# Ones in TensorE's pauses, pinned casts, and a residual kept in accumulators: a two-layer trunk in fp32

## Chip, cores and metric

One core of one Trainium2 chip runs the whole program. The metric is device time in microseconds (us) of one execution; a shorter time is better.

## The reference, cut to what matters

Two layers on a prompt of 1024 tokens and a sample of 512, 1024 features wide. Layer 0 mixes tokens with a Fourier transform, layer 1 with attention; each is followed by a SwiGLU. The change touches layer 0 alone.

```python
def rms_norm(x, g):
    y = xf * lax.rsqrt(jnp.mean(xf * xf, axis=-1, keepdims=True) + EPS)
    return (y * g).astype(x.dtype)
...
def fourier_mixer(x, g, w):
    h = rms_norm(x, g).reshape(b, s, N_FGROUPS, FGROUP_DIM)
    mixed = jnp.real(jnp.fft.fft2(h, axes=(1, 3), norm="ortho"))
    return mixed.reshape(b, s, d) @ w
...
def swiglu_ffn(x, g, w_gate, w_up, w_down):
    h = rms_norm(x, g)
    return (jax.nn.silu(h @ w_gate) * (h @ w_up)) @ w_down
...
x = x + fourier_mixer(x, ...)      # layer 0; attention_mixer in layer 1
x = x + swiglu_ffn(x, ...)
```

## The kernel before

Tokens are worked on in three blocks of 512 columns: block 0 is the sample ("s"), blocks 1 and 2 the prompt ("p"). Activations are transposed: features on the 128 partitions, in eight chunks `dc` or `n`, tokens along the free dimension. Each fp32 operand is split into a high part (a cast to fp32r) and a low part (the source minus the cast), and each product is three matmuls, high by high, high by low and low by high (`mm3`, L244 to L246). So each weight of 128x1024 passes through four steps (`weights`, L248): SP issues its load into a `raw` buffer, ScalarE (ACT) casts it, GpSimd (POOL) subtracts, TensorE (PE) uses both parts. There are few `raw` buffers; a load waits until POOL's subtraction has freed one. The projection's weights (`folded`, L586) pass through one step more: POOL adds and subtracts the two halves of a chunk of `wf` (L590, L591) ahead of the cast.

The start runs in these stages. `load_rows("s")` loads the sample. `lead` (L1079) is the sample's mixer: squares and their sums on ACT, the reciprocal root on VectorE (DVE) in `rsqrt` (L257, here 15 small operations, with the square root's iterations written out), then four quarters of features. In each, rows of tokens are scaled and combined (ACT L424, DVE L426, cast L237), multiplied by the transform `mat_s` on PE, and turned over the group's features (`dd`, `alt`, L498, L405). The transform's matrices come in one staging buffer; `mat_p`, the prompt's, comes in it too, by a DMA that ACT issues in the first microsecond, and ACT casts it in four parts (L1088). `lead` also begins four folds, and with fold 2 the small matrix `w64`.

`follow` (L1098) is the projection: for each of eight chunks 25 matmuls of 256 or 258 columns into four PSUM tiles, which DVE adds to the chunk of the residual (L624, L625, L629). `new_residual` (L294) writes the chunk to `xres` in DRAM, squares it on ACT (L305) and adds the squares up on DVE (L306). After the last chunk `rstd_cols` (L276) sums over partitions by products with ones (L280) and calls `rsqrt`; `normed` (L311) spreads the factors over partitions by four products of a diagonal with ones (L288, L289), loads each chunk of `xres` back, multiplies it on DVE into PSUM (L324) and splits it with the gain (ACT L240, DVE L241) into `h`.

Then `ffn(0, 0)` runs 22 steps `fc`: eight chunks of gate, eight of up (48 matmuls of 512 columns each step with `part`), the SwiGLU, and eight chunks of down, whose sums DVE adds to accumulators in SBUF; at the first step these are loaded from `xres` (L663). Beside it, `weave` (L1028) runs an auxiliary stage, here the prompt's mixer `x_0`. It alternates between the two by the costs that each `yield` states. Later stages pair the other blocks' SwiGLU with attention in the same way.

What `weave` lays down is the program; a scheduler of the framework sets from it a fixed order of instructions for each engine, by its own estimates of when each could start. `keep_in_program_order`, which the change uses, pins an instruction to its place in the program's order. The chip then runs each engine's list strictly in order, and an instruction that waits holds up all behind it. DMA issues stand in the lists of SP and ACT alike.

## Time and profile before

| | us |
|---|---|
| median of 3 runs | 3134.45 |
| lowest, highest | 3128.28, 3134.93 |
| profiled execution | 3136.16 |
| its span | 3134.4 |
| PE busy in the span | 3005.0 (96%) |
| DVE, POOL, ACT busy | 1656.4, 1325.6, 1243.9 |

The span is what the profiler shows of the execution; busy times are sums over each engine's instructions. An engine's idle time is shown in front of the instruction that ended it, with the event that released it. PE's clock is shown twice: as the clock that was granted in a stretch, and in how closely products follow each other.

### The profile page before, as it was taken

The page shows a single profiled execution, that of the slowest core. Times are in us where ns is not written, and L with a number is a line of the kernel's source. Part 1 is how long each engine was busy: PE and PEld are TensorE (multiplying, and loading weights), DVE is VectorE, ACT ScalarE, POOL GpSimd, SP SyncE. Part 2 cuts the span into 40 slices and gives each one's busy share as a digit, 9 for nine tenths or more (in the row PEclk, how much of TensorE's full clock was granted, in tenths as well). Part 3 has the DMA queues.
Part 4 walks back from the last instruction along what each step waited for, and adds up shares of the span by engine and source line. Part 5 has one row for each costly group of instructions (what it writes and reads, how often), then busy time and mean ns, then how long its engine had stood idle before and what let it go on. Part 6 is the DMA issues. An engine that isn't in the chain of part 4 may idle for free. (4 is left out here: it accounts for less than half of the span.)

```text
span 3134.4 us, 37508 instructions
## 1 busy us (share of the span) xinstructions
PE 3005.0 (96%) x14382; PEld 2471.0 (79%) x14382; DVE 1656.4 (53%) x2974; ACT 1243.9 (40%) x1807; POOL 1325.6 (42%) x616
## 2 busy tenths in 40 slices
PE   5699999999999999999999999999999999999999
PEld 5687788888887778888878788778787777777777
DVE  5664455453466553453455466665337455655556
ACT  5443323233266632233334377777424222222221
POOL 3444734444233454444443322222546644554452
PEclk9799999999999999999999999999999999999999
DMA  5424553333223454343343311111645511111111
GB/s 181 157 81 119 178 173 103 115 117 95 82 91 99 164 174 133 125 132 105 98 155 92 103 58 65 58 58 58 203 141 176 182 54 54 48 48 53 54 48 61
DMA packets 131385, 336.13 MB, mean 107 GB/s; under 512 B 15699, under 2 KB 23891, under 8 KB 130693
## 3 DMA queue, kind: packets, MB, share of 16 engines
q1 hardware_dynamic: 129476, 322.68, 32.2%
q10 hardware_dynamic: 1440, 6.85, 0.6%
q0 software_dynamic: 288, 4.19, 0.4%
q8 instruction: 113, 1.85, 0.2%
q14 instruction: 68, 0.55, 0.1%
HBM read 286.48 MB, written 47.19 MB: 106 GB/s over the span
## 5 line engine op out<-in xcount | busy, mean ns | idle before, releaser
L238 POOL TENSOR_TENSOR w<-raw,w 128x1024 fp32r<-128x1024 f32 (+1 forms) x463 | 1093.4, 2371 | 1632.9 <-ACT w L237 1596.3
L237 ACT CAST w<-raw 128x1024 fp32r<-128x1024 f32 (+1 forms) x463 | 479.2, 1038 | 754.8 <-PE c L246 357.2
L664 DVE TENSOR_TENSOR acc<-c,acc 128x512 f32<-128x512 f32 x704 | 482.8, 689 | 476.2 <-PE c L246 473.0
L244 PE MATMUL g<-h,w 128*128 128x512 f32 x1408 | 557.2, 396 | 6.8 <-DVE h L241 6.5
L246 PE MATMUL g<-h,w 128*128 128x512 f32 x1408 | 553.7, 394 | 0.0
L245 PE MATMUL g<-h,w 128*128 128x512 f32 x1408 | 552.9, 393 | 0.0
L244 PE MATMUL c<-mid,w 128*128 128x512 f32 x1056 | 419.9, 399 | 17.3 <-DVE acc L664 15.2
L245 PE MATMUL c<-mid,w 128*128 128x512 f32 x1056 | 414.5, 393 | 0.7 <-DVE mid L238 0.7
L246 PE MATMUL c<-mid,w 128*128 128x512 f32 x1056 | 413.9, 392 | 0.0
L771 DVE TENSOR_TENSOR acc<-c,acc 128x512 f32<-128x512 f32 x352 | 240.9, 689 | 192.8 <-PE c L246 192.0
L244 PEld LDWEIGHTS g<-h,w 128*128 128x128 f32 x1408 | 266.1, 189 | 59.7 <-DVE h L241 6.8
L246 PEld LDWEIGHTS g<-h,w 128*128 128x128 f32 x1408 | 266.0, 189 | 55.1 <-POOL w L238 0.3
L245 PEld LDWEIGHTS g<-h,w 128*128 128x128 f32 x1408 | 266.2, 189 | 52.1
L244 PEld LDWEIGHTS c<-mid,w 128*128 128x128 f32 x1056 | 198.6, 189 | 80.1 <-DVE acc L664 27.4
L246 PEld LDWEIGHTS c<-mid,w 128*128 128x128 f32 x1056 | 199.0, 188 | 41.5
L245 PEld LDWEIGHTS c<-mid,w 128*128 128x128 f32 x1056 | 199.5, 189 | 40.2 <-DVE mid L238 1.8
L244 PE MATMUL c<-h,w 128*128 128x512 f32 x480 | 189.9, 396 | 1.7 <-ACT h L237 1.7
L245 PE MATMUL c<-h,w 128*128 128x512 f32 x480 | 188.5, 393 | 1.3 <-POOL h L238 1.3
L246 PE MATMUL c<-h,w 128*128 128x512 f32 x480 | 187.2, 391 | 0.0
L983 DVE TENSOR_REDUCE col<-a 128x1 f32<-128x1024 f32 (+1 forms) x96 | 100.4, 1045 | 125.9 <-PE a L246 125.7
L987 ACT ACTIVATE p<-a,col,rqc 128x1024 f32<-128x1024 f32 (+1 forms) x96 | 102.3, 1066 | 65.7 <-DVE col L984 65.3
L689 ACT ACTIVATE t<-g 128x512 f32<-128x512 f32 x88 | 52.6, 598 | 175.4 <-PE g L246 175.1
(299 smaller groups left out, 4749.9 us busy)
## 6 DMA issues: line engine op xcount, KB each, us to landing
raw<-in_down_dram SPq DMA_DIRECT2D x110, 512.0 KB, 3.7
raw<-in_gate_dram SPq DMA_DIRECT2D x88, 512.0 KB, 3.7
raw<-in_up_dram SPq DMA_DIRECT2D x88, 512.0 KB, 3.8
raw<-in_qkv_dram SPq DMA_DIRECT2D x36, 512.0 KB, 3.5
t<-xres SPq DMA_DIRECT2D x64, 256.0 KB, 4.2
xres<-t SPq DMA_DIRECT2D x48, 256.0 KB, 3.7
acc<-xres SPq DMA_DIRECT2D x48, 256.0 KB, 4.3
raw<-in_wo_dram SPq DMA_DIRECT2D x24, 512.0 KB, 4.3
```

Source lines behind the costliest of these rows:

```text
L237: act.copy(hi, src)
L238: eng.tensor_tensor(lo, src, hi.bitcast(F32), op=ALU.subtract)
L244: pe.matmul(out, lh, rh, start=first, stop=False)
L245: pe.matmul(out, lh, rl, start=False, stop=False)
L246: pe.matmul(out, ll, rh, start=False, stop=last)
L664: dve.tensor_tensor(acc[dc], ps, acc[dc], op=ALU.add)
L689: act.activation(s, ga, AF.Silu)
L771: dve.tensor_tensor(acc, ps, acc, op=ALU.add)
L983: dve.tensor_reduce(st[:, 0:1], s_in, op=ALU.max, axis=AX.X)
L987: act.activation(p, s_in, AF.Exp, bias=st[:, 1:2], scale=rqc[:, gq, h : h + 1], accum_out=sm[:, 0:1])
```

## The change

It has eight parts, all in the stages ahead of, and at, the first SwiGLU's first step.

1. A dummy Square on ACT at the very start.
2. `busy(n)`: n products of a 128x128 tile of ones with itself, whose results nothing reads, pinned: 64 behind `load_rows("s")`, 10 behind the last chunk of the projection, 12 behind the column sums.
3. `rsqrt` keeps its iterate in an SBUF column and drops four copies.
4. The DMA of `dft_p` (2 MB) moves from ACT's queue at the start to SP's behind the first combination; the gate is a one-element copy on DVE into the staging buffer (`after`). The four casts of `mat_p` and the folds move to later, stated places `k` of `lead`, where their casts are pinned; the first fold has such a gate too.
5. Folds 4 to 7 are begun in the projection ahead of their chunk, and the gate, up and down weights of step 0 at its chunks 5, 6 and 7.
6. Block 0's residual stays in the accumulators of `ffn(0, 0)` (`resident`): nothing is written to `xres` nor read back.
7. Its norm is one DVE operation per chunk (accumulator by gain by factor, into SBUF), ACT's cast, and POOL's subtraction.
8. In step 0 gate and up alternate chunk by chunk, and `x_0` is advanced four times instead of once ahead of `follow`.

In the rows of order below, a name ends in the number of its tile, `<-` separates what is written from what is read.

**ACT at the sample's last combination** (`comb`, the cast that the fourth quarter's products wait for; `eo` are casts for the projection's operand, x_p prompt rows), before:

```order
L237 CAST xrs_526<-t_524 1x256
L424 ACTIVATE a_495<-x_136,r_s 128x256
L240 ACTIVATE spec_s<-g_471,gains 128x2
L355 DMA x_p_626<-in_rows_p_dram 128x1024
L237 CAST comb_494<-a_495 128x2x256
L237 CAST eo_196<-c_501 128x256
L237 CAST eo_196<-c_502 128x256
```

and now, where w_525 is the fourth fold:

```order
L457 ACTIVATE a_555<-x_138,r_s 128x256
L241 ACTIVATE spec_s<-g_526,gains 128x2
L238 CAST xrs_588<-t_586 1x256
L238 CAST eo_257<-c_561 128x256
L238 CAST eo_257<-c_562 128x256
L635 CAST w_525<-raw_521 128x1024
L238 CAST comb_554<-a_555 128x2x256
```

The fourth fold's cast has come to stand directly ahead of the combination's.

**POOL in the projection** (L590 and L591, now L629 and L630, are the add and subtract of a fold; L238 and L636 the low part of a weight; w_970 and w_885 the last chunk's), before:

```order
L591 TENSOR_TENSOR raw_874<-raw_873 128x512
L238 TENSOR_TENSOR w_878<-raw_874,w_878 128x1024
L590 TENSOR_TENSOR raw_920<-raw_919 128x512
L591 TENSOR_TENSOR raw_920<-raw_919 128x512
L238 TENSOR_TENSOR w_924<-raw_920,w_924 128x1024
L590 TENSOR_TENSOR raw_966<-raw_965 128x512
L591 TENSOR_TENSOR raw_966<-raw_965 128x512
L238 TENSOR_TENSOR w_970<-raw_966,w_970 128x1024
L238 TENSOR_TENSOR w_1101<-raw_1099,w_1101 128x1024
L238 TENSOR_TENSOR w_1131<-t_1141,w_1131 128x2x256
L238 TENSOR_TENSOR w_1106<-raw_1104,w_1106 128x1024
```

and now (w_794 and w_800 are folds 4 and 5, the w of two pieces belong to the prompt's mixer):

```order
L636 TENSOR_TENSOR w_794<-raw_790,w_794 128x1024
L636 TENSOR_TENSOR w_800<-raw_796,w_800 128x1024
L629 TENSOR_TENSOR raw_881<-raw_880 128x512
L629 TENSOR_TENSOR raw_837<-raw_836 128x512
L630 TENSOR_TENSOR raw_837<-raw_836 128x512
L630 TENSOR_TENSOR raw_881<-raw_880 128x512
L239 TENSOR_TENSOR w_744<-t_754,w_744 128x2x256
L239 TENSOR_TENSOR w_744<-t_759,w_744 128x2x256
L636 TENSOR_TENSOR w_841<-raw_837,w_841 128x1024
L239 TENSOR_TENSOR w_767<-t_777,w_767 128x2x256
L239 TENSOR_TENSOR w_767<-t_782,w_767 128x2x256
L636 TENSOR_TENSOR w_885<-raw_881,w_885 128x1024
```

The folds no longer alternate one by one, and four of the prompt's subtractions have come in between.

**ACT between the last chunk's square and the norm's diagonals** (L305, now L330, squares a chunk; L288, now L308, makes a diagonal; w_1101, w_1106 and w_1111 are gate, up and down of step 0 and w_1339 the gate of step 1), before:

```order
L237 CAST w_1106<-raw_1104 128x1024
L305 ACTIVATE a_1008<-t_973 128x512
L237 CAST w_1111<-raw_1109 128x1024
L237 CAST w_1131<-t_1146 128x2x256
L424 ACTIVATE c_1161<-x_p_626,r_p 128x256
L424 ACTIVATE c_1250<-x_p_626,r_p 128x256
L237 CAST w_1339<-raw_1337 128x1024
L237 CAST w_1160<-t_1170 128x2x256
L237 CAST w_1160<-t_1175 128x2x256
L237 CAST xrs_1191<-t_1187 1x256
L424 ACTIVATE c_1250<-x_p_626,r_p 128x256
L288 ACTIVATE t_1036<-ident,rs_1011 128x128
```

and now (w_1002, w_1041, w_1082 and w_1427 in their place):

```order
L330 ACTIVATE a_1036<-acc_788 128x512
L276 CAST w_1002<-raw_1000 128x1024
L330 ACTIVATE a_1077<-acc_788 128x512
L276 CAST w_1041<-raw_1039 128x1024
L330 ACTIVATE a_1129<-acc_788 128x512
L238 CAST xrs_1231<-t_1227 1x256
L276 CAST w_1082<-raw_1080 128x1024
L276 CAST w_1427<-raw_1425 128x1024
L308 ACTIVATE t_1167<-ident,rs_1132 128x128
L308 ACTIVATE t_1170<-ident,rs_1132 128x128
```

The cast of step 1's gate, which stood well ahead of the diagonals, now stands right in front of them, behind that of down.

The diff, cut to its core:

```diff
+    act.activation(col(1), ones[:, 0:1], AF.Square)
...
+    def busy(n):
+        o = bankg()
+        for _ in range(n):
+            pinned(pe.matmul(o[:, 0:P], ones, ones, start=True, stop=True))
+    def after(dst, src):
+        dve.tensor_copy(dst[0:1, 0:1], src[0:1, 0:1])
...
+        pinned(act.copy(flat[:, 0], raw)) if early else act.copy(flat[:, 0], raw)
+        pool.tensor_tensor(flat[:, 1], raw, flat[:, 0].bitcast(F32), op=ALU.subtract)
...
-        v, ti, a, z = (scr[:, k * n : (k + 1) * n] for k in range(4))
-        vs, zs = col(n), col(n)
+        v, ti, a = (scr[:, k * n : (k + 1) * n] for k in range(3))
+        z = col(n)
         dve.tensor_scalar(v, x, scale, EPS, op0=ALU.mult, op1=ALU.add)
         dve.tensor_scalar(ti.bitcast(I32), v.bitcast(I32), 1, None, op0=ALU.logical_shift_right)
         dve.tensor_scalar(z.bitcast(I32), ti.bitcast(I32), -1.0, MAGIC, op0=ALU.mult, op1=ALU.add)
-        dve.tensor_copy(vs, v)
-        dve.tensor_copy(zs, z)
         for k in range(3):
-            dve.tensor_tensor(a, z, zs, op=ALU.mult)
-            dve.scalar_tensor_tensor(a, a, -0.5, vs, op0=ALU.mult, op1=ALU.mult)
-            if k < 2:
-                dve.scalar_tensor_tensor(z, a, 1.5, zs, op0=ALU.add, op1=ALU.mult)
-                dve.tensor_copy(zs, z)
-            else:
-                dve.scalar_tensor_tensor(y, a, 1.5, zs, op0=ALU.add, op1=ALU.mult)
+            dve.tensor_tensor(a, v, z, op=ALU.mult)
+            dve.scalar_tensor_tensor(a, a, -0.5, z, op0=ALU.mult, op1=ALU.mult)
+            dve.scalar_tensor_tensor(z if k < 2 else y, a, 1.5, z, op0=ALU.add, op1=ALU.mult)
...
+        if first and not resting:
+            resting.append(True)
+            busy(12)
...
+        if not stays:
+            sp.dma_start(xres[b][:, dc, :], piece)
...
+        if b in resident:
+            for dc in range(NC):
+                x = tmp()
+                dve.scalar_tensor_tensor(x, resident[b][dc], gain[:, dc : dc + 1], r, op0=ALU.mult, op1=ALU.mult)
+                split(h[:, 0, dc], h[:, 1, dc], x, eng=pool)
+            got["h"] = h
+            return
...
-        split(flat[:, 0], flat[:, 1], f.rearrange("p k n -> p (k n)"), eng=pool)
-        return w
-    def mixer_projection(seq, done, ready=()):
+        f = f.rearrange("p k n -> p (k n)")
+        pinned(act.copy(flat[:, 0], f))
+        pool.tensor_tensor(flat[:, 1], f, flat[:, 0].bitcast(F32), op=ALU.subtract)
+        yield
+    ahead, begun = [], []
+    def begin_fold(n, tag, later=None):
+        begun.append(folded(n, tag, later))
+        ahead.append(next(begun[-1]))
...
+            if two:
+                w, _ = folded(n, "wX")
+            else:
+                w = ahead.pop(0)
+                for m in (4, 5) if n == 0 else (n + 5,) if n < 3 else ():
+                    cur[0] = "XF"[m % 2]
+                    begin_fold(m, "wF")
+                cur[0] = "F"
+                if n in (1, 2, 4, 5):
+                    next(begun.pop(0))
+                if n >= 5:
+                    early.append(weights_by((t["gate"], t["up"], t["down"])[n - 5][0, 0]))
+                    first[n - 5] = next(early[-1])
+                if n >= 6:
+                    next(early[n - 6])
...
+                if not two and n == NC - 1:
+                    busy(10)
...
+        here = b in resident
+        acc = resident.pop(b) if here else accumulators()
...
+            if here and fc == 0:
+                wg, wu, wd = (first[i] for i in range(3))
+            else:
+                wg, wu, wd = (weights(t[v][layer, fc]) for v in ("gate", "up", "down"))
             ga, up = bankg(), bankg()
             for dc in range(NC):
                 part(wg, h, ga, dc)
+                if here and fc == 0:
+                    part(wu, h, up, dc)
...
     load_rows("s")
+    busy(64)
...
-    act.dma_start(stage[:, 2056:6168], t["dft_p"])
...
-            if k in (2, 4, 6, 8):
-                cur[0] = "X"
-                ahead.append(folded(len(ahead), "wX"))
-            if k in (3, 5, 7, 9):
-                c, h = divmod((k - 3) // 2, 2)
-                act.copy(m_p[c][:, h], stage[:, 2056 + 2056 * c + 1028 * h : 2056 + 2056 * c + 1028 * (h + 1)])
-            if k == 5:
-                cur[0] = "X"
+            if k == 2:
+                after(stage, got_s["comb"])
+                sp.dma_start(stage[:, 0:4112], t["dft_p"])
+            cur[0] = "X"
+            if k in (3, 7, 11, 15):
+                begin_fold(len(ahead), "wX", None if ahead else got_s["comb"])
+            if k in (6, 10, 14, 18):
+                next(begun.pop())
+            if k in (8, 9, 12, 13):
+                c, h = divmod((8, 9, 12, 13).index(k), 2)
+                pinned(act.copy(m_p[c][:, h], stage[:, 2056 * c + 1028 * h : 2056 * c + 1028 * (h + 1)]))
+            if k == 16:
...
-        yield from mixer_projection("s", got_s, ahead)
+        yield from mixer_projection("s", got_s)
+        next(early[2])
+        early.clear()
...
-    next(x_0)
+    for _ in range(4):
+        next(x_0)
```

## Rows read from the trace of the kernel before

**Rows 1.** The table of windows: for each stretch of the span its length and the busy time (and count of instructions) of each engine, the mean granted clock of PE, the DMA engines' share and rate; the last row is the sum.

```profile
0.00:28.90 28.90, 0.02 (x1) 0.02 (x1) 11.20 (x33) 10.93 (x16) 11.64 (x13) 1.00 0.65 244
28.90:72.00 43.10, 39.46 (x206) 33.57 (x206) 25.85 (x59) 28.25 (x64) 12.30 (x8) 0.92 0.44 151
72.00:104.00 32.00, 27.39 (x200) 26.83 (x200) 20.70 (x75) 14.51 (x26) 19.62 (x12) 0.89 0.61 203
104.00:135.80 31.80, 11.20 (x43) 9.29 (x43) 24.78 (x64) 16.23 (x31) 13.15 (x8) 0.56 0.57 184
135.80:152.00 16.20, 16.18 (x63) 13.01 (x63) 5.50 (x14) 5.13 (x8) 3.65 (x2) 0.81 0.07 14
152.00:3134.40 2982.40, 2910.76 (x13871) 2388.30 (x13870) 1568.33 (x2733) 1168.81 (x1664) 1265.30 (x574) 1.00 0.33 104
sum 3134.40, PE 3005.01 PEld 2471.03 DVE 1656.37 ACT 1243.86 POOL 1325.65; mean PE 500.83 PEld 411.84 DVE 276.06 ACT 207.31 POOL 220.94
```

**Rows 2.** The timeline of ACT in the opening: start, duration (of all that a row groups), engine and line, operation, tiles and shapes, count; in brackets the idle time before and what ended it.

```profile
19.36 2.00 ACT L1088 CAST mat_p<-stage 128x1028 fp32r<-128x1028 f32 x2 [0.96 <-DMA stage<-in_dft_p_dram]
...
25.02 0.47 ACT L424 ACTIVATE a<-x,r_s 128x256 f32<-128x256 f32 x1
25.43 0.39 ACT L237 CAST xrs<-t 1x256 fp32r<-1x256 f32 x1
```

**Rows 3.** The timeline of DVE in the opening.

```profile
14.91 0.15 DVE L262 TENSOR_SCALAR c<-s_s 128x4 f32<-128x4 f32 x1
...
17.80 0.16 DVE L274 SCALAR_TENSOR_TENSOR r_s<-c,col 128x4 f32<-128x4 f32 x1
...
25.92 1.88 DVE L238 TENSOR_TENSOR xrs<-t,xrs 1x256 fp32r<-1x256 f32 x1
```

**Rows 4.** The timeline of PE, from the first product to the end of the first gate and up step.

```profile
28.88 0.58 PE L244 MATMUL g<-mat_s,comb 128*128 128x258 f32 x1 [28.88 <-ACT comb L237]
...
42.42 0.42 PE L245 MATMUL g<-mat_s,comb 128*128 128x258 f32 x1
42.63 0.42 PE L246 MATMUL g<-mat_s,comb 128*128 128x258 f32 x1
...
43.42 0.28 PE L244 MATMUL g<-mat_s,comb 128*128 128x256 f32 x1
43.54 0.28 PE L245 MATMUL g<-mat_s,comb 128*128 128x256 f32 x1
...
63.05 0.39 PE L244 MATMUL g<-mat_s,comb 128*128 128x258 f32 x1 [0.33 <-ACT comb L237]
...
68.36 0.28 PE L246 MATMUL g<-mat_s,comb 128*128 128x256 f32 x1
...
72.56 0.51 PE L244 MATMUL g<-eo,w 128*128 128x258 f32 x2 [0.80 <-ACT eo L237]
...
103.33 0.28 PE L246 MATMUL g<-eo,w 128*128 128x256 f32 x1
107.45 1.46 PE L280 MATMUL c<-ones,ss 128*128 128x1 f32 x8 [3.84 <-DVE ss L306]
...
120.55 1.92 PE L289 MATMUL c<-t,ones 128*128 128x128 f32 x8
...
135.82 0.80 PE L244 MATMUL g<-h,w 128*128 128x512 f32 x1 [6.54 <-DVE h L241]
...
151.53 0.39 PE L245 MATMUL g<-h,w 128*128 128x512 f32 x1
151.76 0.39 PE L246 MATMUL g<-h,w 128*128 128x512 f32 x1
```

**Rows 5.** The loads of the folded weights (wf): SP's queue where they are issued, POOL's first operation on each (three rows each, from the timelines of the two), and the rate of all DMA in 40 equal slices of the first 145 us.

```profile
5.37 12.31 SPq L589 DMA_DIRECT2D raw<-in_wf_dram  x2
...
27.56 10.73 SPq L589 DMA_DIRECT2D raw<-in_wf_dram  x2
...
81.70 0.33 SPq L589 DMA_DIRECT2D raw<-in_wf_dram  x1
...
14.52 1.59 POOL L590 TENSOR_TENSOR raw<-raw 128x512 f32<-128x512 f32 x1 [13.20 <-DMA raw<-in_wf_dram]
...
41.63 1.28 POOL L590 TENSOR_TENSOR raw<-raw 128x512 f32<-128x512 f32 x1 [0.20 <-DMA raw<-in_wf_dram]
...
86.12 1.28 POOL L590 TENSOR_TENSOR raw<-raw 128x512 f32<-128x512 f32 x1 [0.89 <-DMA raw<-in_wf_dram]
...
GB/s 95 396 413 399 431 163 0 52 120 0 38 108 73 201 411 277 216 346 1 15 134 72 23 314 214 315 272 260 208 281 216 303 205 50 193 205 132 5 0 0
```

**Rows 6.** The groups of POOL's instructions in the first 240 us: busy time and mean ns of one, then the idle time before them and its releasers.

```profile
L238 POOL TENSOR_TENSOR w<-raw,w 128x1024 fp32r<-128x1024 f32 x24 | 57.2, 2387 | 63.5 <-ACT w L237 63.4
L238 POOL TENSOR_TENSOR w<-t,w 128x512 fp32r<-128x512 f32 x16 | 20.4, 1284 | 32.9 <-ACT w L237 32.8
```

**Rows 7.** The timelines of ACT (three rows) and DVE (one row) from the prompt's squares to the norm of the sample's block.

```profile
74.49 1.05 ACT L365 ACTIVATE raw<-x_p 128x1024 f32<-128x1024 f32 x1
...
106.08 0.59 ACT L305 ACTIVATE a<-t 128x512 f32<-128x512 f32 x1
...
119.45 0.97 ACT L288 ACTIVATE t<-ident,rs 128x128 f32<-128x128 f32 x3
...
124.80 1.31 DVE L324 TENSOR_TENSOR g<-c,t 128x512 f32<-128x512 f32 x2 [1.02 <-DMA t<-xres]
```

More of the change, by code (lines that the diff above doesn't have):

```diff
@@ L290, in in_rows, with accumulators, new_residual @@
         return r
-    ss, rstd = {}, {}
-    def new_residual(b, dc, piece, out=None):
+    ss, rstd, resident = {}, {}, {}
+    def accumulators():
+        halves = [acc_tile("acc", [4, TB], F32) for _ in range(2)]
+        return [a[:, i] for a in halves for i in range(4)]
+    def new_residual(b, dc, piece, out=None, stays=False):
         if out is not None:
@@ L425, in combine @@
                 for k, w in enumerate(scal(cb)):
-                    dve.scalar_tensor_tensor(half(dst, k), x(cb), w, half(fa, i), op0=ALU.mult, op1=ALU.add)
+                    ins = dve.scalar_tensor_tensor(half(dst, k), x(cb), w, half(fa, i), op0=ALU.mult, op1=ALU.add)
+                    if two and q == 1 and c == 0:
+                        pinned(ins)
             if not two:
@@ L683, in ffn @@
             for dc in range(NC):
-                part(wu, h, up, dc)
+                if not (here and fc == 0):
+                    part(wu, h, up, dc)
                 one()
@@ L760, in ffn_pair @@
         for b in blocks:
[L761 to L762 removed]
+            accs[b] = accumulators()
         credit = [0.0]
```

48 lines of the change are left out of this document (25 added, 23 removed).

## The prediction

> **What bounds the kernel now.** I read the table of windows by stage first [rows 1]. After 152 us TensorE (PE) is busy 2910.8 of 2982.4 us at granted clock 1.00: only 71.6 us are idle there, and the change removes no product. Before 152 us PE is busy 94 of 152 us, at 0.92, 0.89, 0.56 and 0.81 of its clock: this is where time can be won. The timelines of ScalarE (ACT), VectorE (DVE) and PE [rows 2 to 4] then show three waits: up to 28.88 us for the first combination; inside the projection; and from its last product at 103.33 to the first FFN product at 135.82, 32.5 us with only 11.2 us of products in 104 to 135.8. The clock is in the spacing of the products: products of 256 to 258 columns follow each other by 0.21 us at 42.42 and by 0.12 at 43.42, the half (1.2 GHz) and the full level (2.4 GHz).
>
> I walk the new order from event to event with durations from rows, and compare one state: all 48 products of the first gate and up step and the 42 prompt-mixer products ahead of their end are done. Before that is at about 152.0 (the last of the 48 starts at 151.76 [rows 4]).
>
> **Start.** Before, ACT makes two casts of mat_p (2.00 us together) and those of two folds ahead of its first scaling of a row at 25.02, though r_s is there at 17.96 [rows 2, 3]. After, that scaling stands right behind the squares. The four copies gone from rsqrt are worth 4 x 0.2 = 0.8, so r_s comes at 17.2. From the scaling to the first product took 28.88 - 25.02 = 3.86, of which the xrs subtraction on DVE held 1.88, 1.5 more than the cast of the same tile took on ACT; POOL's fold, beside which it ran, is gone from there. With the small DVE operations between: first real product at about 20.4. The dummy Square only moves the table load into the wait for the rows: DVE's L262 stood behind DVE's own work, so I cost it at nothing.
>
> The 64 products of ones fill PE from 1.1. Four calls of this shape (eight records) took 1.92 at 120.55, at the half level [rows 4], 0.48 each, and I take 0.23 at the full one. If the clock rises only after 14 us of work, as between 28.88 and 43 here, they end at 1.1 + 14 + 35 x 0.23 = 23.2; sooner if it rises sooner; if never, at 31.8. The first two cost nothing at the end, since the next step binds.
>
> **Folds 0 to 3.** The DMA of dft_p and fold 0 are now gated by the first combination (about 21.3). 2.6 MB at the 396 to 431 GB/s of the opening [rows 5] take 6.3, with some 2 of latency to 29.7. Each fold's buffer then passes from load to POOL and back: a load took 41.63 - 37.96 = 3.7 (the pair of issues from 27.56 ends at 38.29, the second being its last 0.33) or 86.12 - 81.70 = 4.4, the add and the subtract 1.28 each [rows 5]. So 6.4 per fold: POOL's subtract ends at 32.2, 38.6, 45.0 and 51.4. The fourth fold's cast (1.05) is pinned ahead of the last combination's cast on ACT, so that combination's first product comes at 51.4 + 1.05 + 0.6 = 53.1 against 63.05 before: 10 us won. The last mat_s product follows 5.6 later as before, 58.6 against 68.36, and the projection could begin 4.2 behind it, at 62.9 against 72.56.
>
> **Folds 4 to 7.** Here part is lost again. Fold 4's buffer is one that the squares of the prompt's rows use. Before, ACT ended its eighth square at 75.54, 12.5 behind the last combination's product [rows 7]; now two casts stand with them: 53.1 + 12.5 + 2.1 = 67.7. With a load, 72. From there POOL has fold 4's add and subtract (2.6), the low parts of folds 4 and 5 (2 x 2.39), all of folds 6 and 7 (10.0) and four prompt subtractions (4 x 1.28) [rows 6]: 22.5, with one uncovered cast 23.5, so the last fold is ready at 95.5. PE alone would need 200 products x 0.12 = 24 from 62.9, that is 87; POOL binds. The last chunk's 25 products (3.0) end at 98.5 to 100; I take 99 against 103.6: of the 10 us, 4.6 are left.
>
> **Norm.** Gone are eight writes and eight loads of xres and eight loads of acc; the first product of DVE's norm stood at 124.80 behind such a load [rows 7]. Also gone is the wait of PE for seven chunks of h at DVE: each chunk now has its own wait. The sum of squares alone, behind ACT's square (0.6), DVE's add (0.65, as the operation of its size at 124.80), the one-column products (1.5), 12 rsqrt operations (2.4), four diagonals (0.97 for three, so 1.3) and four products (1.0 to 1.9) [rows 4, 7], would give the factors near 108. Another chain is later: the up load is issued when POOL has done the last fold (95.5), lands at 99.4, cast 100.5, POOL 102.9; that frees the buffer for the second step's gate, which lands at 106.8, and its cast stands on ACT ahead of the four diagonals, to 107.9. The factors come at 110.2. DVE's product (0.65) and ACT's cast (0.6) give the first FFN product at about 112 against 135.82. POOL's subtraction of each chunk (1.28) keeps ahead of the six products that use it (6 x 0.23 = 1.37).
>
> The 22 products of ones at the end cost at most 22 x 0.48 = 10.6, in a pause of some 13 us (99 to 112); nothing, if the prompt-mixer products behind them fit too, 12 x 0.12 to 0.21 = 1.4 to 2.5. They just do.
>
> **Step 0.** 48 x 0.23 + 12 x 0.12, with the mixer's own waits (about 3), is 15.6 at the full clock; a start at the half level as before (granted 0.81 over 16.2 us [rows 1], so 0.19 x 16.2) would add 3. Mostly at the full level, since the ones stand right before it, I take 17.5: the state is reached at 129.5 against 152.0. The gain is 22.5. Behind it nothing is removed but the table loads and DMAs; order and buffers shift a little, and I put ±5 on that.
>
> **Sum.** The profiled execution took 3136.16 us (span 3134.4), 1.7 above the median of 3134.45. 3136.16 - 22.5 = 3113.7, on the median's level **3112**. Bounds of the terms: projection end 98 to 100; loads 3.7 to 4.4, six in series (0 to +4); step 0 15.6 to 18.6; later stages ±5. Together 3104 to 3122.
>
> **A rule against it.** A DVE operation with two SBUF inputs ran 1.88 us at 25.92 beside a POOL subtraction, and the change puts more subtractions on POOL. The Trainium skill (SBUF — State Buffer, section "SBUF: two separate sides") says that the two share a port pair as an exclusive lock, so that the later one is fully blocked. The row agrees with it. By rule, DVE's L331 and the xrs subtraction could each wait out a POOL operation of 2.39 in the norm; the gate chain covers about 2 of these 4.8, so the sum by it would be near 3115 rather than 3112; that lies inside the forecast's own range, and has no chance of its own. Of the loads the Trainium skill (DMA: Bandwidth & Descriptors, "Anatomy of one DMA — SWDGE (gpsimd) path") gives a fit, 2.0 us plus bytes/436e3, estimated 3.2 us for these 512 KB; it is for another issuing path, the rows show 3.7 to 4.4, and by it six loads would put the time at 3109.
>
> **The rivals.**
> - Larger gain: the fold loads overlap more than I read from the order (two buffers in flight), so that neither the fourth fold nor the gate chain binds. PE's 206 products of 28.9 to 72 at the pace of 72 to 104 (27.39/200) take 28 instead of 39.5, so the last combination comes near 48, the FFN near 106: 10 us more, about 3102. For it: the loads have a DMA share of only 0.44 to 0.61 beside them.
> - The ones don't lift the clock: the first product comes at 31.8, and the mixer at the full spacing later still reaches the last combination at 56 to 58, 3 to 5 behind my 53.1; 3116. The change then doesn't do what it says in its first part.
> - No change: the stages after 152 give back the 22 us. They would need 94 idle us instead of 71.6, a third more. For it: four steps of the prompt mixer and three weights are pulled forward, which shifts every later buffer. Against: those stages are bound by PE. About 3134.
> - Slower: the six serial loads (folds 1 to 3, fold 4, up, second gate) each take what the first fold took, 14.52 - 5.37 = 9.15 [rows 5], since prompt rows, xT and weights share the queue. That is 5.4 x 6 = 33 more, 3145. It is slower from 8.5 per load on (4.8 x 6 = 29). Against it: loads under traffic at 81.70 took 4.4.
>
> **How the numbers follow.** Forecast 0.64; larger gain 0.14; ones without effect 0.04; no change 0.10; slower 0.08. 0.2% (6.3 us) is about what a measurement of this kernel can tell from no change. The range takes in the forecast, the ones without effect and most of the larger gain, with some room towards no change: 3097 to 3128. Faster 0.82, same 0.10, slower 0.08.
>
> **What would show it.** Right: products of ones from 1 to about 20 us, the last combination's first product near 53, the fourth fold's cast just ahead of it on ACT; PE's pauses in the projection ended by POOL's low parts; the diagonals on ACT right behind a weight cast that a load released; first FFN product near 112; idle time behind the first step near 72 us. Wrong: a first FFN product later than 125, folds apart by 9 instead of 6.4, or an idle sum behind step 0 over 85.

## The result, and the profile after

| | before | after |
|---|---|---|
| median of 5 runs each, us | 3131.46 (3128.28 to 3134.93) | 3117.2 (3108.85 to 3118.71) |
| ratio, 95% interval | | 0.9948 [0.9933, 0.9962] |
| profiled execution, its span, us | 3136.16, 3134.4 | 3117.2, 3115.4 |

The kernel is faster by half a per cent. The two spans differ by 19.0 us; the profiled execution of before lies 4.7 above its median of five, so by medians it is 14.3. Before's median over five lies 3.0 below the 3134.45 that the prediction started from.

The state that the prediction compares, the 48 products of the first gate and up step and the 42 of the prompt's mixer all done, comes at 140.0 instead of 152.0: 12.0 us are won by then, where 22.5 were forecast. Here are the table of windows of after, cut at the milestones that answer to [rows 1] (the last two rows overlap), and the timeline of PE that answers to [rows 4].

```profile
0.00:19.60 19.60, 16.77 (x129) 16.58 (x129) 6.87 (x29) 7.33 (x13) 0.70 (x6) 1.00 0.50 191
19.60:73.67 54.07, 46.74 (x207) 39.94 (x207) 27.69 (x62) 30.87 (x66) 23.15 (x15) 0.65 0.53 185
73.67:110.90 37.23, 27.89 (x200) 27.10 (x200) 29.58 (x84) 19.07 (x33) 24.34 (x15) 0.86 0.33 104
110.90:122.60 11.70, 9.37 (x75) 8.81 (x75) 6.34 (x20) 6.27 (x12) 7.09 (x3) 1.00 0.40 128
122.60:144.07 21.47, 19.37 (x93) 15.60 (x94) 12.44 (x24) 12.15 (x21) 13.61 (x10) 1.00 0.10 27
140.00:3115.40 2975.40, 2907.89 (x13872) 2387.51 (x13870) 1551.17 (x2683) 1167.68 (x1670) 1269.10 (x577) 1.00 0.33 104
```

```profile
1.06 16.77 PE L260 MATMUL g<-ones 128*128 128x128 f32 x128 [1.06 <-DVE ones L216]
19.60 0.39 PE L245 MATMUL g<-mat_s,comb 128*128 128x258 f32 x1 [1.77 <-ACT comb L238]
...
22.55 0.41 PE L245 MATMUL g<-mat_s,comb 128*128 128x258 f32 x1 [1.73 <-ACT comb L238]
...
27.11 0.42 PE L246 MATMUL g<-mat_s,comb 128*128 128x258 f32 x1
27.33 0.42 PE L247 MATMUL g<-mat_s,comb 128*128 128x258 f32 x1
...
60.22 0.50 PE L245 MATMUL g<-mat_s,comb 128*128 128x258 f32 x1 [2.27 <-ACT comb L238]
...
68.65 0.41 PE L247 MATMUL g<-mat_s,comb 128*128 128x256 f32 x1
...
73.67 0.39 PE L245 MATMUL c<-eo,w 128*128 128x258 f32 x1 [0.26 <-ACT eo L238]
...
98.14 0.55 PE L245 MATMUL g<-eo,w 128*128 128x258 f32 x1 [6.73 <-DVE acc L695]
...
107.16 0.39 PE L247 MATMUL g<-eo,w 128*128 128x258 f32 x1 [1.03 <-POOL w L636]
...
109.78 0.28 PE L247 MATMUL g<-eo,w 128*128 128x256 f32 x1
...
122.60 0.73 PE L245 MATMUL g<-h,w 128*128 128x512 f32 x2 [1.07 <-ACT h L238]
...
139.85 0.28 PE L247 MATMUL a<-mat_p,w 128*128 128x256 f32 x1
```

The milestones in a table, before, forecast and after, in us (FFN is the SwiGLU of block 0, step 0 its first step):

| | before | forecast | after | behind the forecast |
|---|---|---|---|---|
| first real product | 28.88 | 20.4 | 19.60 | -0.8 |
| last combination's first product | 63.05 | 53.1 | 60.22 | +7.1 |
| projection's first product | 72.56 | 62.9 | 73.67 | +10.8 |
| projection's last product | 103.33 | 99 | 109.78 | +10.8 |
| first FFN product | 135.82 | 112 | 122.60 | +10.6 |
| both product groups done | 152.0 | 129.5 | 140.0 | +10.5 |

So the head start of 9.3 us is gone when the projection starts, 1.1 later than before, and when the projection ends the kernel is 6.5 later than before; it stays that far behind the forecast to the end of step 0. All that is won by 140 is won between the projection's last product and the end of step 0: that stretch took 48.7 us before and takes 30.2. Behind it, PE is idle for 67.5 us (2975.40 less 2907.89) where it was 71.6 behind 152.

### The profile page after: what moved, and what is told of

The parts are those of the page before. It is cut to its first block, busy times and chain, and to the rows that moved or that the text cites. A ratio compares the mean times of both kernels' runs of the same rounds, so it can differ in the third digit from the quotient of the medians.

```text
span 3115.4 us, 37725 instructions
## 1 busy us (share of the span) xinstructions
PE 3024.0 (97%) x14554; PEld 2492.2 (80%) x14554; DVE 1630.1 (52%) x2888; ACT 1240.3 (40%) x1806; POOL 1334.4 (43%) x624
## 5 line engine op out<-in xcount | busy, mean ns | idle before, releaser
L277 POOL TENSOR_TENSOR w<-raw,w 128x1024 fp32r<-128x1024 f32 x346 | 826.7, 2399 | 1234.2 <-ACT w L276 1200.1
L276 ACT CAST w<-raw 128x1024 fp32r<-128x1024 f32 x346 | 362.2, 1048 | 490.3 <-PE c L247 263.4
L239 POOL TENSOR_TENSOR w<-raw,w 128x1024 fp32r<-128x1024 f32 (+1 forms) x101 | 228.2, 2266 | 340.2 <-ACT w L238 319.1
L238 ACT CAST w<-raw 128x1024 fp32r<-128x1024 f32 (+1 forms) x101 | 100.2, 1000 | 202.1 <-PE a L247 86.6
```

Source lines behind the costliest of these rows:

```text
L238: act.copy(hi, src)
L239: eng.tensor_tensor(lo, src, hi.bitcast(F32), op=ALU.subtract)
L276: pinned(act.copy(flat[:, 0], raw)) if early else act.copy(flat[:, 0], raw)
L277: pool.tensor_tensor(flat[:, 1], raw, flat[:, 0].bitcast(F32), op=ALU.subtract)
```

## Experiments

Each is an edit of the kernel after, except for norm_alone, which adds two parts to the kernel before. The parts are numbered as in the section on the change. Each median has its range and its ratio to the kernel before run beside it, with the 95% interval. The median of before was 3129.75 to 3134.41 us in these groups of runs, so the ratios are to be compared; that of after is 0.9948 [0.9933, 0.9962]. Milestones are from one profiled execution each; up to 4 us between two of them can come without any edit (last section).

**The ones at the start left out.**

```diff
-    busy(64)
+    busy(0)
```

> The 64 products of ones behind the load of the sample's rows are left out. Theory A (the clock in the mixer: the ones hold the full level only until about 23 us, since PE's pauses ahead of each combination let it fall again, so they are worth little): first real product at 19.6 as with them, first quarter at the half spacing, last combination's first product 0 to 3 us later than 60.2, time 3117 to 3120. Theory B (the ones are what brought the gain of the opening): the mixer ends 8 us later or more, time 3124 or more.

Measured: 3121.21 us (3114.2 to 3123.25), ratio 0.9961 [0.9948, 0.9973]. The first product came at 19.17, the projection at 75.42 and the first FFN product at 124.07, 1.5 us later than in after; that is no more than two profiles of the same order of work differ by (last section), and the ratio's interval overlaps with after's. So the ones at the start are worth little, if anything. Two things are to be seen in the mixer. The timelines of ACT and PE show the last combination held, and by what:

```profile
58.71 1.04 ACT L635 CAST w<-raw 128x1024 fp32r<-128x1024 f32 x1 [3.43 <-POOL raw L630]
59.66 0.58 ACT L238 CAST comb<-a 128x512 fp32r<-128x512 f32 x1
```

```profile
60.30 0.58 PE L245 MATMUL g<-mat_s,comb 128*128 128x258 f32 x1 [4.71 <-ACT comb L238]
```

PE is through with all the rest (5.50 us busy in 50 to 60), and waits 4.71 us for a cast that stands on ACT behind the fourth fold's, which waits for POOL. And the windows of the two kernels, 20 to 30 us, after's two rows first, then this kernel's:

```profile
20.00:25.00 5.00, 3.27 (x14) 2.43 (x13) 2.71 (x7) 1.71 (x4) 0.00 (x0) 0.78 0.72 240
25.00:30.00 5.00, 4.95 (x19) 4.13 (x20) 2.30 (x6) 2.27 (x6) 0.42 (x1) 0.50 0.68 286
```

```profile
20.00:25.00 5.00, 3.78 (x13) 2.75 (x12) 2.32 (x6) 1.87 (x4) 0.00 (x0) 1.00 0.77 270
25.00:30.00 5.00, 4.95 (x21) 4.41 (x21) 2.60 (x7) 2.10 (x6) 0.85 (x1) 1.00 0.61 256
```

With the ones, the granted clock is at the full level to the first row's products, then falls to the half (0.50), behind pauses of 1.77 and 1.73 us ahead of the first two combinations. Without them it reads 1.00 there, but PE is as busy with about as many products: they follow each other by 0.21 us, too. This trace has no record of the clock ahead of 34.5 us, and the table shows 1.00 where it has none, as it does for before up to 28.90, where PE did next to nothing [rows 1]. So the spacing of the products must be read with the granted clock; the 0.92 of before in 28.90 to 72.00 is too high, since its products were still 0.21 apart at 42.42 [rows 4].

**The ones behind the projection left out.**

```diff
-            busy(12)
+            busy(0)
...
-                    busy(10)
+                    busy(0)
```

> The 10 and the 12 products of ones around the column sums are left out. If they keep the clock up for the first gate and up step: the prompt's products and the first FFN products stand at the half spacing (0.43 for 512 columns) for some microseconds, the step's first gate and up (122.6 to 137.8) end 3 to 4 us later, time 3120 to 3121. If the step waits for POOL's subtractions and the prompt's products anyway: no change, 3116 to 3118.

Measured: 3121.75 (3115.85 to 3122.34), 0.996 [0.9947, 0.9972]. The first product of down (c from mid) came at 147.3 where it is at 144.07 with them, though the projection began 1.6 earlier (72.05). The granted clock was 0.59 in 108 to 122 and 0.94 in 122 to 140; with them it is 1.00 in both. They do what they are there for, and are worth 3 to 5 us there in these two profiles; the ratios' intervals overlap.

**Eight more products of ones per quarter row of the sample's mixer.**

```diff
-            xrs = fixed_row(q)
+            xrs = fixed_row(q); busy(0 if two else 8)
```

> Eight more products of ones ahead of each quarter of the sample's mixer (32 in all), to fill PE's pause there. Theory A (the half level in the mixer is what delays it): granted clock near 1.00 instead of 0.65 between 20 and 70 us, the last combination before 56 instead of 60.2, first FFN product at 116 to 119 instead of 122.6, time 3110 to 3114. Theory C (the chain of folds, 8.9 us apart, and the fourth fold's cast on ACT ahead of the last combination set the mixer's end): the clock is up, but the last combination stays at 59 to 60 and the time at 3116 to 3118.

Measured: 3116.13 (3112.79 to 3118.62), 0.9947 [0.9935, 0.996]. The windows of 20 to 70 us, after's row first, then this kernel's, and a row of its PE timeline:

```profile
20.00:70.00 50.00, 43.14 (x178) 36.52 (x178) 26.20 (x58) 27.26 (x56) 21.49 (x14) 0.63 0.51 181
```

```profile
20.00:70.00 50.00, 46.18 (x265) 39.90 (x264) 27.72 (x63) 32.80 (x69) 23.41 (x15) 0.81 0.58 210
```

```profile
55.27 0.39 PE L245 MATMUL g<-mat_s,comb 128*128 128x258 f32 x1 [0.85 <-ACT comb L238]
```

With more products PE's pace rises, and the last combination comes 5 us sooner, with the fold's cast ahead of it as before; the projection (68.10) gains 5.6 and the first FFN product (116.59) 6.0. That the clock alone did this isn't shown. The edit also changed the order of PE, ACT and DVE in the mixer, from about 33 us on. And free_and_ones (below) has the same order on all four engines up to 305 us, but after a combination at 55.77 its projection began at 71.36 and its FFN at 120.54. What both show is the combination, 2 to 5 us sooner than in five kernels with after's order up to there (58.00 to 60.22). The median moves by 1.1, which is no difference: the profiled execution took 3112.79, the shortest of its five.

**The fourth fold's cast behind the last combination.**

```diff
-            if k in (6, 10, 14, 18):
+            if k in (6, 10, 14, 19):
```

> The fourth fold's pinned cast is moved from ahead of the last combination to one step later, behind the first half of the last quarter's products. Theory A: the last combination comes 2.3 us earlier (the pause of PE at 60.2), the folds behind are not later, time 3115 to 3117. Theory C: it comes 5 or more earlier, time 3110 to 3113. If the fourth fold is then late for its own chunk of the projection: no gain, 3117 to 3119.

Measured: 3115.93 (3113.39 to 3119.07), 0.9951 [0.9937, 0.9964]. The combination came at 59.05 instead of 60.22, the projection at 74.33 and the FFN at 123.95. PE no longer waits for the combination; it comes to it only then, since its products up to there are 0.21 apart. So the cast alone isn't the bound: PE's own pace is a second one, in this profile 1.2 us shorter. Nothing of the 1.2 is left at the projection.

**The old opening in the new kernel.** dft_p loads at the start, the first folds and the casts of mat_p stand where they did before and aren't pinned; all the rest stays. Not pinned are then also the first four casts of the prompt's folds.

```diff
-        pinned(act.copy(dst, raw))
+        act.copy(dst, raw)
...
-        pinned(act.copy(flat[:, 0], f))
+        act.copy(flat[:, 0], f) if n < 4 else pinned(act.copy(flat[:, 0], f))
...
-    row_in("s", stage[:, 7128:7644])
+    row_in("s", stage[:, 7128:7644]); act.dma_start(stage[:, 2056:6168], t["dft_p"])
...
-            if k in (3, 7, 11, 15):
-                begin_fold(len(ahead), "wX", None if ahead else got_s["comb"])
-            if k in (6, 10, 14, 18):
+            if k in (3, 5, 7, 9):
+                begin_fold(len(ahead), "wX")
...
```

> The changed kernel with the old opening: dft_p is loaded by ACT's queue at the start, folds 0 to 3 and the casts of mat_p come early and unpinned, as before; ones, resident residual, norm, early weights and step 0 stay as changed. Theory N (the opening gains nothing by the projection's start, all of the gain is made between the projection's end and the first FFN product): projection starts at 72 to 74, first FFN product within 3 of 122.6, time within 3 of 3117. Rival O (the 9 us won at the first product are kept): first FFN product 8 or more later, time 3125 or more.

Measured: 3110.49 (3104.43 to 3113.56), 0.9934 [0.9919, 0.995]. The first product came at 27.52, 8 us later than in after, the last combination at 63.83, the projection at 75.11, only 1.4 later, and the first FFN product at 119.23, 3.4 sooner. The new opening has bought next to nothing by the projection. The whole got no slower without it, rather faster (the intervals overlap); in the prompt's projection, where four casts are free here, PE waits 3.7 us for POOL's low parts, where after waits 8.2 (free_prompt_casts, below).

**Parts 6 and 7 alone (resident residual, norm without PSUM) in the kernel before.**

```diff
+    resident = {}
...
+        if b in resident:
+            for dc in range(NC):
+                x = tmp()
+                dve.scalar_tensor_tensor(x, resident[b][dc], gain[:, dc : dc + 1], r, op0=ALU.mult, op1=ALU.mult)
+                split(h[:, 0, dc], h[:, 1, dc], x, eng=pool)
+            got["h"] = h
+            return
...
-                new_residual(b, n, x)
+                new_residual(b, n, x, stays=not two)
...
```

> The kernel before with parts 6 and 7 alone: block 0's residual stays in the accumulators, and its norm is DVE, ACT and POOL without PSUM; no ones, old opening, old weights, old order of gate and up. Theory N: the pause from the projection's last product to the first FFN product falls from 32.5 to 13 to 18 us, first FFN product at 117 to 121, time 3116 to 3121. Rival: it needs the early weights and the clock as well; the pause stays over 24 us, time 3124 to 3130.

Measured: 3129.62 (12 runs, 3123.84 to 3134.94), 0.9993 [0.9982, 1.0005]. The timeline of PE shows why:

```profile
112.25 1.87 PE L280 MATMUL c<-ones,ss 128*128 128x1 f32 x8 [10.05 <-DVE ss L313]
...
127.66 1.22 PE L244 MATMUL g<-h,w 128*128 128x512 f32 x2 [1.49 <-ACT h L237]
```

The projection ended near 102, but the column sums started 4.8 us later than before [rows 4]: on ACT the squares stand behind casts of weights that wait for their loads (the last square at 110.88). The first FFN product is at 127.66, 8 us sooner than before, and at the half level (granted 0.50 in 108 to 122, 0.68 in 122 to 140), so of the 8 us 4.4 are left at the first product of down.

**All but parts 6 and 7.**

```diff
-                xs.append(tmp() if two else resident[b][n])
+                xs.append(tmp())
...
-                new_residual(b, n, x, stays=not two)
+                new_residual(b, n, x)
...
-        here = b in resident
-        acc = resident.pop(b) if here else accumulators()
+        here = layer == 0 and b == 0
+        acc = accumulators()
...
```

> The changed kernel without parts 6 and 7: block 0's residual goes to DRAM and back, the norm reads it chunk by chunk and works through PSUM, the accumulators are loaded from DRAM. Theory M (the gain in the norm needs parts 5, 6 and 7 together: DVE's eight products and their loads stand on the path again): first FFN product 6 to 10 us later than 122.6, first product of down 6 to 10 later than 144.1, time 3122 to 3127. Rival: the early weights and the ones alone carry it, first product of down within 3, time 3116 to 3120.

Measured: 3131.69 (11 runs, 3126.1 to 3141.63), 0.9994 [0.9984, 1.0004]. PE's timeline:

```profile
140.67 0.79 PE L245 MATMUL g<-h,w 128*128 128x512 f32 x1 [5.93 <-DVE h L242]
```

Neither half is worth anything measurable alone, and both together 0.5%. In each of the two profiles the chain that was left in place sets the first FFN product: with the old norm it is DVE's h behind loads of xres, without the early weights it is ACT's squares behind their casts.

**One advance of the prompt's rows instead of four.**

```diff
-    for _ in range(4):
+    for _ in range(1):
```

> The prompt's mixer is advanced by one step ahead of the projection instead of four. Theory L (the prompt's small DVE operations and POOL subtractions inside the projection hold it up): the pauses of PE in the projection (0.7, 6.7 and 1.0 us) fall below 4 in sum, first FFN product 3 to 6 us earlier than 122.6; the prompt's products then lie behind it, so that the time is 3112 to 3118. Rival: the pull forward is what pays, time 3121 or more.

Measured: 3122.9 (9 runs, 3118.59 to 3127.15), 0.9978 [0.9968, 0.9989]. The projection ran from 73.06 to 105.08, without the pause of 6.73 that after has in it for DVE, and the first FFN product came at 120.45, sooner than in after. But the prompt's last product of mat_p came at 256.9 (249.8 in after) and the column sums of its second norm, the one ahead of its SwiGLU, at 443.6 (435.51): what is pulled ahead costs the sample's FFN some 2 us and saves the prompt 8 later.

**DVE's smallest operations on ACT.** The two of `masked` and the negation, which run beside POOL's low parts.

```diff
-        dve.tensor_tensor(m[:, 0:1], r[:, c : c + 1], mask, op=ALU.mult)
-        dve.tensor_scalar(m[:, 1:2], m[:, 0:1], -1.0, None, op0=ALU.mult)
+        act.activation(m[:, 0:1], r[:, c : c + 1], AF.Copy, scale=mask)
+        act.activation(m[:, 1:2], m[:, 0:1], AF.Copy, scale=-1.0)
...
-        dve.tensor_scalar(neg, r, -1.0, None, op0=ALU.mult)
+        act.activation(neg, r, AF.Copy, scale=-1.0)
```

> Five small operations on the prompt's factors (128x1 and 128x8) go from DVE to ACT. In the changed kernel three of them took 2.07 and 2.36 us at 86.4 to 90.7 beside two POOL subtractions. Theory L (these stalls and what they hold up on DVE cost time): the 4.2 us are gone, PE's pause of 6.7 us in the projection falls to 3 or less, first FFN product at 118 to 121, time 3112 to 3116. Theory P (POOL's chain of folds binds, DVE's stall is beside it): POOL's last fold still ends at 107, first FFN product within 1 of 122.6, time within 2 of 3117.

Measured: 3118.85 (7 runs, 3112.33 to 3126.8), 0.9965 [0.9951, 0.9979]. What it was about, in after's timelines of DVE and of POOL:

```profile
86.37 2.07 DVE L405 TENSOR_TENSOR m<-r_p,mask 128x1 f32<-128x1 f32 x2
88.36 2.36 DVE L421 TENSOR_SCALAR neg_p<-r_p 128x8 f32<-128x8 f32 x1
90.64 0.20 DVE L406 TENSOR_SCALAR m<-m 128x1 f32<-128x1 f32 x2
```

```profile
85.97 4.72 POOL L636 TENSOR_TENSOR w<-raw,w 128x1024 fp32r<-128x1024 f32 x2 [1.16 <-ACT w L635]
```

While POOL makes two low parts, from 85.97 to 90.69, two DVE operations on one column take 2.07 us together and one on eight columns takes 2.36; as soon as POOL is done with them, two on one column take 0.20. The Trainium skill (SBUF — State Buffer, section "SBUF: two separate sides") has DVE and POOL share a port pair as an exclusive lock, which blocks the later one for the other's whole instruction; these rows agree. With these moved, the two stalls are gone, but PE still paused 5.91 us for the accumulators (L695), behind the prompt's rows on DVE, and POOL's chain of folds took 23.5 us (84.95 to 108.41) where it takes 24.8 in after. The median shows no gain. This profile is of the longest of the seven executions, 3126.8, with the projection at 76.70 and the first FFN product at 128.45, so its milestones don't tell what the stalls cost.

**The casts of the prompt's folds not pinned.**

```diff
-    def folded(n, tag, later=None):
+    def folded(n, tag, later=None, freed=False):
...
-        pinned(act.copy(flat[:, 0], f))
+        act.copy(flat[:, 0], f) if freed else pinned(act.copy(flat[:, 0], f))
...
-                w, _ = folded(n, "wX")
+                w, _ = folded(n, "wX", freed=True)
```

> The casts of the prompt's eight folds (projection of blocks 1 and 2, 300 to 440 us) are no longer pinned; all else is the changed kernel, and the order is the same up to there. In the changed kernel PE waited there seven times for POOL's low parts, 8.2 us in sum; before, 1.5. Theory G (this new wait gives back part of the gain): these waits fall below 3 us, the second norm comes 3 to 6 us earlier than 435.5, time 3111 to 3115. Rival: PE waits for something else there, time 3116 to 3119.

Measured: 3109.28 (3103.46 to 3113.54), 0.9921 [0.9908, 0.9935], the largest gain of a single edit. Of the waits of PE from 290 to 445 us, where the prompt's projection lies, those for POOL's low parts, and this kernel's longest (what waited, for whom: us in total, times, longest): before, after, this kernel.

```profile
PE c L246 <- POOL w L238: 1.5, 2, 1.1
```

```profile
PE c L247 <- POOL w L636: 8.2, 7, 2.3
```

```profile
PE c L245 <- DVE acc L728: 4.8, 2, 4.0
...
PE c L247 <- POOL w L636: 1.2, 1, 1.2
```

And the place in after, in the timelines of POOL and PE:

```profile
333.25 2.40 POOL L277 TENSOR_TENSOR w<-raw,w 128x1024 fp32r<-128x1024 f32 x1 [7.35 <-ACT w L276]
335.61 2.33 POOL L636 TENSOR_TENSOR w<-raw,w 128x1024 fp32r<-128x1024 f32 x1
```

```profile
338.00 0.39 PE L247 MATMUL c<-eo,w 128*128 128x258 f32 x1 [2.29 <-POOL w L636]
```

`folded` serves both projections, so the pin that was meant for the lead fixed the prompt's casts too. POOL idles 7.35 us for a weight's cast, then makes that weight's low part, and the fold that PE waits for comes behind it. With the casts free these waits fall by 7.0 us, though one for DVE's accumulators (4.8) appears; all of PE's waits in the window fall from 14.1 to 7.8. From the prompt's last product of mat_p to the column sums of its second norm it takes 178.6 us (247.40 to 426.00) instead of 185.7 (249.85 to 435.51). So the pins give back some 7 us there, and the median falls by 7.9, though the two intervals just touch.

**Two combinations.** `best` has the old opening, no pins on the folds of "wX" at all, 98 products of ones at the start and 5 per quarter; `free_and_ones` has free prompt casts and 8 per quarter. The edit of best against old_opening:

```diff
-            xrs = fixed_row(q)
+            xrs = fixed_row(q); busy(0 if two else 5)
...
-        act.copy(flat[:, 0], f) if n < 4 else pinned(act.copy(flat[:, 0], f))
+        act.copy(flat[:, 0], f) if tag == "wX" else pinned(act.copy(flat[:, 0], f))
...
-    busy(64)
+    busy(98)
```

> The changed kernel with the old opening, 98 products of ones at the start (to the first product), 5 ahead of each quarter of the sample's mixer, and the prompt's casts unpinned. If the clock in the mixer and the prompt's casts are worth what the runs with each alone suggest (last combination's first product at 60 to 62 instead of 63.8 with the old opening, waits for POOL in the prompt's projection below 3 us): second norm at 422 to 426, time 3104 to 3108. If they don't add up: 3109 to 3113.

> The prompt's fold casts unpinned and eight products of ones ahead of each quarter of the sample's mixer, with the new opening; the two edits that won alone. If they add up (6.0 us at the first product of down, and the waits for POOL in the prompt's projection): first product of down at 136 to 139, second norm at 420 to 423, ratio to the kernel before 0.990 to 0.991. If the mixer's gain is given back behind it, as with the ones alone: ratio 0.9915 to 0.9925.

Measured: best 3107.73 (4 runs, 3106.68 to 3109.94), 0.9919 [0.9905, 0.9932]; free_and_ones 3107.39 (3106.76 to 3112.7), 0.9919 [0.9906, 0.9933]. Both beat before and after, and neither is apart from free_prompt_casts alone: no gain of the ones in the mixer shows on top. The milestones that were expected were missed. In best the projection began at 77.98 (75.11 in old_opening) and the column sums of the second norm came at 429.00; in free_and_ones the first FFN product is at 120.54, as without the ones per quarter (120.11), the first product of down at 142.01 and the second norm at 429.75.

## Why the prediction was right, and which step failed

The time and its side were right: 3117.2 for 3112, within the forecast's own 3104 to 3122. The gain was 14.3 us for 22.5. Of the signs of being wrong that the prediction named, one came about: the folds are 9 us apart, not 6.4. Point by point:

- **Start** was right: 19.60 for 20.4. The ones were done at 17.83.
- **Folds 0 to 3 is the step that failed**, in the sentence "So 6.4 per fold", and again in "The first two cost nothing at the end, since the next step binds". The timeline of POOL shows the four folds and what lies between the first two; ACT's shows what the first fold's cast stands behind, and SP's queue the issue of the fourth fold's load:

```profile
29.58 1.28 POOL L629 TENSOR_TENSOR raw<-raw 128x512 f32<-128x512 f32 x1 [28.27 <-DMA raw<-in_wf_dram]
...
35.99 2.36 POOL L636 TENSOR_TENSOR w<-raw,w 128x1024 fp32r<-128x1024 f32 x1 [3.70 <-ACT w L635]
38.44 1.27 POOL L629 TENSOR_TENSOR raw<-raw 128x512 f32<-128x512 f32 x1
...
47.34 1.29 POOL L629 TENSOR_TENSOR raw<-raw 128x512 f32<-128x512 f32 x1
...
56.09 1.28 POOL L629 TENSOR_TENSOR raw<-raw 128x512 f32<-128x512 f32 x1 [2.63 <-DMA raw<-in_wf_dram]
```

```profile
33.16 0.37 ACT L238 CAST eo<-c 128x256 fp32r<-128x256 f32 x1 [0.27 <-PE c L533]
...
34.38 0.59 ACT L238 CAST comb<-a 128x512 fp32r<-128x512 f32 x1
34.86 1.06 ACT L635 CAST w<-raw 128x1024 fp32r<-128x1024 f32 x1
```

```profile
49.88 0.33 SPq L628 DMA_DIRECT2D raw<-in_wf_dram  x1
```

The first is at 29.58, as forecast with 29.7. The next are 8.86, 8.90 and 8.75 behind each other, and the second and third wait for no load: POOL goes to them straight from the low part of the fold before, which waited 3.70 us for a cast on ACT, and that cast is pinned behind a combination, which stands behind casts that wait for PE. So the mixer's rows set these folds. The fourth waits 2.63 us for its load, which took 6.2 from its issue for the forecast's 3.7 to 4.4, with the prompt's rows on their way beside it. The last fold's cast in turn holds the last combination. The forecast counted load, add and subtract, and left out the low part and the cast's place: three folds at 8.8 instead of 6.4 are the 7.1 us that the last combination is behind. And the rows themselves are slow: products of 258 columns at 27.11 and 27.33 are 0.22 apart, and the granted clock is 0.63 over 20 to 70 us. A kernel with the same order up to there, free_prompt_casts, bears this out: its granted clock was 0.83 in 30 to 40 us where after has 0.67, and its folds are 6.27, 7.68 and 10.14 apart. So the first interval is the forecast's where PE is quicker, and the fourth fold waits for its load again, 3.29 us. late_fold_cast and no_start_ones show the two chains that end at the last combination: with the cast out of the way PE comes to it at 59.05 without a pause, and with the cast in place the wait is up to 4.71 where the rest is done sooner. How the lost time divides between the two isn't settled, since the chain passes through both.
- **The step from the last combination to the projection** failed, too: "The last mat_s product follows 5.6 later as before". It followed 8.4 later (68.65), where before had 5.3 (68.36), since the granted clock was 0.52 in 60 to 70 us; before it was 1.00 there. That is most of the further 3.7 us that the projection's start is behind the forecast. The ones at the start were done long before, and the forecast gave the mixer's later rows the old pace without a reason.
- **Folds 4 to 7** was right in its size, not in its start nor in what PE waited for. POOL went from 82.28 to 107.11 in 24.8 us, for 23.5, and the last chunk's products waited 1.03 for its last low part. But PE's longest pause there, 6.73 ahead of 98.14, was ended by DVE's addition (L695), which stood behind the prompt's rows that part 8 pulled forward; the forecast gave these time on POOL and none on DVE. one_next, with three of the four advances gone, has no such pause, and its projection takes 32.0 us for after's 36.1.

```profile
82.28 1.28 POOL L629 TENSOR_TENSOR raw<-raw 128x512 f32<-128x512 f32 x1 [10.62 <-DMA raw<-in_wf_dram]
...
104.73 2.38 POOL L636 TENSOR_TENSOR w<-raw,w 128x1024 fp32r<-128x1024 f32 x1
```

- **Norm** was right in its chain and its size: 15.5 us from the last fold to the first FFN product, for 16.5. SP's queue and ACT's timeline show the up load, its cast, the second gate's load (issued at 114.41), its cast and the diagonals in a row; the diagonals, at 119.14, come as late as before (119.45 [rows 7]), and the first FFN product follows 3.5 us behind them, where it took 16.4.

```profile
107.14 0.33 SPq L272 DMA_DIRECT2D raw<-in_up_dram  x1
```

```profile
110.89 1.04 ACT L276 CAST w<-raw 128x1024 fp32r<-128x1024 f32 x1 [3.61 <-DMA raw<-in_up_dram]
...
118.19 1.04 ACT L276 CAST w<-raw 128x1024 fp32r<-128x1024 f32 x1 [3.68 <-DMA raw<-in_gate_dram]
119.14 1.38 ACT L308 ACTIVATE t<-ident,rs 128x128 f32<-128x128 f32 x4
```

- **Step 0**: 17.4 for 17.5, at granted 1.00. no_end_ones shows that the late ones hold that level.
- **The ±5 behind it** held by luck, and hid two large terms of opposite sign. Four advances of the prompt's rows gain some 8 us at its second norm (one_next); the pinned casts of its folds lose some 7 (free_prompt_casts). The sum has neither, and the section on the change places the pins in the lead alone, though `folded` serves both projections. By spans the stages behind step 0 gain 7.0, of which 4.7 is the profiled execution of before being above its median.
- **The sum** is nearer than the gain: these 2.3 us by medians and the 12.0 at step 0 make 14.3, 8.2 short of the forecast's 22.5 with nothing behind. 3.0 of the 8.2 don't show in the time, since before's median came out 3.0 lower with two more runs.
- **The rule on the ports** holds in the rows at 86 to 91 us, and small_on_act shows no gain from taking these stalls away. In the norm DVE's L331 took its usual 0.69 us (at 112.47) and the xrs subtraction 1.58 beside POOL (at 113.08), ahead of the gate's cast that the diagonals waited for anyway.
- **The rivals**: none came about whole. "No change" names a mechanism that is there, later stages that give back, at a third of its size and outweighed by what they gain. "Slower" has folds as far apart as it says, but two of the three intervals are not due to loads.

## What to carry over

Follow a chain of loads, casts and subtractions through every engine that it visits, and look for what each instruction stands behind there: a pin ties the chain to the work in front of it, which may be slower than any load. Where two chains end close together, try each alone and both together: here the halves were worth 0.9993 and 0.9994, the whole 0.9948. And list all who call a shared function before costing an edit in it: what it gave back a stage later was half of what the kernel had won. And take an execution's milestones for one throw: compare kernels with the same order first, to see how far they scatter.

## What was not expected of the hardware

- 64 calls of ones kept PE busy from 1.06 to 17.83, and yet the granted clock read 0.78 in 20 to 25 us and 0.50 in 25 to 30, behind two pauses of 1.8 us with products between them; then it went up and down (0.67, 0.67, 0.66 and 0.52 in the four stretches of ten from 30 to 70 us).
- In no_start_ones the granted clock read 1.00 to 30 us, and products of 256 to 258 columns still came every 0.21 us. They came every 0.12 only from 34.95 on; the trace's record of the clock begins at 34.5.
- A DVE operation on 128x8 took 2.36 us beside POOL's subtraction of 128x1024, as long as that itself, while an addition of 128x512 that reads one operand from PSUM took 0.68 beside POOL's additions (91.54), as it does with POOL idle (109.46).
- Two kernels with the same order of work up to 300 us (after and free_prompt_casts), one profile each, had the last combination at 60.22 and 58.00 and the first FFN product at 122.60 and 120.11, with granted 0.63 and 0.73 in 20 to 70 us: differences of 2 us in the opening can come without any edit there. ones_in_mixer and free_and_ones, with the same order up to 305 us, differ by more: 55.27 and 55.77, but 68.10 and 71.36 at the projection and 116.59 and 120.54 at the FFN.
